# Retention steps at fixed distances, the sum of squares later, background work at every fourth step, later last loads

## The chip, the cores and the metric

The kernel runs on one core of one Trainium2 chip, as one launch. The metric is the device time of an execution in microseconds. The engines go by their names in the profile: PE is TensorE, DVE is VectorE, ACT is ScalarE, POOL is GpSimd, SP issues most DMAs.

## The reference

One layer of a streaming encoder on 512 frames of width 2048, in float32 (cut to what matters):

```python
h = rmsnorm(x, norm_gain)
proj = h @ w_in
(aq, ak, av, az, iq, ik, iw, rq, rk, rv, rz, ga, gb) = jnp.split(proj, SPLIT_POINTS, axis=-1)
ik = plain_layernorm(ik)
a_out = dsa_mixer(aq, ak, av, iq, ik, iw, positions, rel_bias) * jax.nn.silu(az)   # top-128 keys
rq, rk = rope(rq, positions), rope(rk, positions) * (R_KEY_DIM ** -0.5)
b_out = retention_mixer(rq, rk, rv, ret_gn_gain) * jax.nn.silu(rz)
merged = jax.nn.sigmoid(ga) * (a_out @ w_a_out) + jax.nn.sigmoid(gb) * (b_out @ w_b_out)
r = x + merged @ w_o
return r + (p_i @ w_ple) * jax.nn.sigmoid(r @ w_ple_gate)      # and a last rmsnorm
```

The retention mixer has 8 heads of width 128. For each head and chunk it takes scores of turned queries and keys with a decay, adds what the state of earlier chunks gives, and normalises each frame's output over the head (a group norm).

## The kernel before

**Matmuls in split parts.** A float32 product is made of reduced-precision matmuls. Every weight block arrives by DMA as `wraw`; ACT copies it into a high part `wh` (L138), and DVE (or POOL in the retention and attention stages) subtracts to get the low part `wl` (L144). A plain gemm (`gemms`, L198 to L200) issues three matmuls of 512 columns for each 128 of the inner dimension; a gate pair (`gemm_pair`, L253 and L254) makes two output blocks with seven products of eight times two matmuls, by a Strassen-like scheme whose moving parts are prepared sums (`hd` in DRAM, 56 tiles).

**Steps set the order.** No scheduler reorders anything: the instructions stand in program order on each engine. After every group of matmuls the code calls `step()`. A step first runs whatever `later(n, f)` has put on that step, then takes one entry of the list `todo`; an entry of `None` does nothing. If the step's entry is `None` or the list is empty, and the number of the step is a multiple of `state["rate"]` (`BG_RATE`, 3 at first), one background piece is issued from `bg`. So the list is a sequence in which work waits for its turn behind what was listed earlier, and `later` is a fixed distance.

**Stages.** The stages around the change, with the steps each gives:

- The first gemm (keys and head weights of the indexer), 32 steps, with x split and the squares of x summed in two accumulators. Then `f_sum` (L449, DVE, adds the two), `f_rnat` (L394, four one-column matmuls `ps_ms` over the partitions, then the reciprocal root), `f_bcast`, `f_keys1` to `f_keys3`, all in `todo`, during seven index gemms of 16 steps each. The index scores follow in the same list, 9 entries for each gemm.
- The values for heads 0 to 3 (64 steps), then heads 0 to 3 of 32 steps each: the queries' gemm (`ps_rq`), their rotation on DVE (L719 to L722), the keys' gemm (`ps_rk`), their rotation. Then the values for heads 4 to 7 and these heads.
- A retention head's twelve further steps run inside the next head's gemms: `scores` (L752, four matmuls that need the rotated keys, then DVE's L754), `keys` (a turn on PE and a copy on ACT), `states` (L775, L777, L779), `values_out` four times (L789, L791), `norm` (statistics on DVE, L796 to L800, and a power on POOL, L801), `scale` (L808, `yn`), `back` (L762 turns `yn` on PE, L817 copies it as `yT`; two steps later SP stores it, L818). They stand in `todo`: 35 entries with their gaps.
- Head 7 makes queries and keys together and calls `x_load(2)` sixteen times: SP loads moving parts of the gates back from `hd` (L832) into tiles that the normalised x lets go. With ten loaded at its start this makes 42 of 56. The last 14 are put on fixed steps after head 7.
- The gate pairs, 56 steps each. The first runs beside the steps of head 7. Later stages are not touched.

**Background.** The pieces are, in order: for 8 pairs of blocks of x a load, a normalisation (L649) and four steps that make the gates' moving parts (L268, L277 to L280) and store them to `hd`; 48 top-k rounds (L606, L607, L609); 160 pieces for the position bias. There are 256 in all. In the gates the rate is 24.

**Tiles.** Most tiles come from one pool of 65 slots of 128 by 512 (`U`). A new tile gets the free slot that was let go first, and its first writer waits until the old tile's last reader is done.

Of the kernel before, what the change touches and what calls it, by code (L numbers as in the profile page):

```python
# [19 lines left out]
NH = 8  # L20
NT = L // 128
# [13 lines left out]
def block_kernel(tc, xT, pT, posb, posq, w_in, w_v, w_ik, w_a, w_b, w_o, w_ple, w_gate,  # L35
# [4 lines left out]
    with contextlib.ExitStack() as ctx:  # L40
# [10 lines left out]
        def U(name, dt=F32):  # L51
            return up.tile([128, L], dt, name=name, tag="u")

        def B(name, dt=F32):
            return bp.tile([128, 1280], dt, name=name, tag="b")

        def P(name):
            return pp.tile([128, L], F32, name=name, tag="p")

        def S(name, n):  # L60
            return sm.tile([128, n], F32, name=name, tag=f"s{n}")

        def tok(t):
            return slice(128 * t, 128 * t + 128)
# [6 lines left out]
        unfinished = {}  # L71
        state = {"raw": 0, "split": 0, "rate": BG_RATE}
        pool_units = []
# [82 lines left out]
        todo = collections.deque()  # L156
# [4 lines left out]
        def later(n, f):  # L161
            if n <= 0:
                return f()
            tick[1] += 1
            heapq.heappush(soon, (tick[0] + n, tick[1], f))
# [176 lines left out]
        for k in range(KT):  # L342
            if k in (1, 2, 4, 8, 12):
                load_to(state["raw"] + 1)
            if k < 10:
                t = U("xk")
                sp.dma_start(t, xT[:, k, :])
                xs.append(t)
            elif k % 2 == 0:
                t = B("xk2")  # L350
# [201 lines left out]
            dve.scalar_tensor_tensor(st[64:128, :], st[64:128, :], -1.0, r_b[64:128, :], op0=OP.mult, op1=OP.mult)  # L552

        N3 = [None] * 3
        todo.extend(N3 * 2 + [f_sum] + N3 + [f_rnat] + N3 * 3 + [f_bcast, None, f_keys1] + N3 * 3 + [f_keys2] + N3 * 2 + [f_keys3] + N3 * 2)
        later(80, f_pos)
        later(96, f_rope1)
        later(104, lambda: f_turns(0))
# [166 lines left out]
        def retention_head(h, vs):  # L725
# [6 lines left out]
            else:  # L732
                i = u_r[h][0][0]
# [24 lines left out]
            def turn(src, n):  # L758

                ps = P("ps_t")  # L760
                for t in range(n):
                    pe.transpose(ps[:, tok(t)], src[:, tok(t)], ident)  # L762
                return ps[:, 0:128 * n]

            def keys(i):
                if i == 0:
                    E["pk"] = turn(sk, 3)
                else:
                    E["kn"] = U("kn")
                    act.activation(E["kn"][:, 0:384], E["pk"], AF.Copy, scale=dect[:, 256:257])  # L770
# [12 lines left out]
            def values_out(t):  # L783
                if t == 0:
                    E["py"] = P("ps_y")
                    E["st"] = S("gst", 24)
                    E["mv"] = S("gmv", 8)
                o = E["py"][:, tok(t)]
                pe.matmul(o, E["at"][:, tok(t)], vs[t][:, hc], start=True, stop=(t == 0))  # L789
                if t:  # L790
                    pe.matmul(o, qd[:, tok(t - 1)], E["s"][:, tok(t - 1)], start=False, stop=True)  # L791
# [20 lines left out]
            def back(i):  # L812
                if i == 0:
                    E["pt"] = turn(E["yn"], NT)
                else:
                    E["yT"] = U("yT")
                    act.activation(E["yT"], E["pt"], AF.Copy, scale=gn[:, h:h + 1])  # L817
                    later(2, lambda: sp.dma_start(yd[h], E["yT"]))  # L818

            todo.extend([None] * 5)  # L820
            todo.extend([scores, lambda: keys(0), None, lambda: keys(1)] + [None] * 3 + [states, None, None])
            todo.extend([lambda t=t: values_out(t) for t in range(NT)])
            todo.extend([None, norm] + [None] * 5 + [scale] + [None] * 5 + [lambda: back(0), None, lambda: back(1)])

        Xh = {n: [None] * 8 for n in PRODUCTS}
        x_wanted = collections.deque((n, k) for n in PRODUCTS for k in range(8))
# [1 line left out]
        def x_load(count):  # L828
            while x_wanted and count:
                n, k = x_wanted.popleft()  # L830
                Xh[n][k] = U("h" + n, F32R)
                sp.dma_start(Xh[n][k].bitcast(F32), x_at[n, k])  # L832
                count -= 1

        for h in range(NH):
            if h % 4 == 0:
                rv = values(u_rv[h // 4], "rv")
            retention_head(h, rv)
        for i in range(len(x_wanted)):
            later(4 + 2 * i, lambda: x_load(1))  # L840
        hparts.clear()
        state["rate"] = BG_RATE2

# [199 lines left out]
        for m in PAIRED:  # L1043
            t = B("sm")
# [18 lines left out]
        for m in range(8):  # L1063
# [13 lines left out]
            if m == 7:  # L1077
                todo.extend([None] * 24)
                for k in range(2):
                    t = U("pk")  # L1080
# [9 lines left out]
        for m in range(MF):  # L1090
            i = u_p[m // 4][0]
# [3 lines left out]
            h, l = loaded[i]  # L1095
# [8 lines left out]
            t = U("pw")  # L1104
# [158 lines left out]
IN_RAWS = 2  # L1263
AHEAD = 4
LOADS = 5
BG_RATE = 3
BG_RATE2 = 24
X_AHEAD = 10
AZ_PAIRED = 4
# [98 lines left out]
```

## Time and profile before

| | us |
|---|---|
| median of three runs | 1810.67 (1810.29 to 1814.06) |
| the profiled execution, its own time | 1809.38 |
| its span in the trace | 1807.6 |
| PE busy | 1752.1 (97%) |
| DVE busy | 1210.6 (67%) |
| ACT busy | 738.1 (41%) |
| POOL busy | 395.4 (22%) |
| mean granted TensorE clock | 0.99 of full speed |

The index gemms run from about 28 us to 104 us of the span, the first values to 155 us, heads 0 to 3 to 257 us, the second values to 305 us, heads 4 to 7 to 404 us, the gate pairs to about 873 us. A row of the waits names the waiting engine, tile and line, then what ended the wait, then the total, the number and the longest in us. A row of a timeline has the start, the duration, the engine, the line, the operation and its shapes; in brackets stands the idle time before it and what ended that.

### The profile page before, as it was taken

To read this page: it belongs to the slowest core of one execution; us is meant where nothing else is said; L and a number is where in the kernel's file an instruction comes from. 1 tells how busy PE (TensorE), PEld (TensorE's weight loads), DVE (VectorE), ACT (ScalarE), POOL (GpSimd) and SP (SyncE) were. 2 spreads that over 40 slices of the span, in tenths; PEclk is the share of its full clock that TensorE was granted. 3 is DMA by queue.
4 is the path that set the end of the run, shared out by engine and by line. 5 is a ranking of instruction groups with operands and counts; after the bars stand their busy time and mean duration, and the time that the engine had idled before them with its cause. 6 is when DMAs were issued, how large, how long until landed. Compare 5 with 4: busy or idle time off the path is not lost. (4 is left out here: it accounts for less than half of the span.)

```text
span 1807.6 us, 23881 instructions
## 1 busy us (share of the span) xinstructions
PE 1752.1 (97%) x8966; PEld 1462.5 (81%) x8966; DVE 1210.6 (67%) x1959; ACT 738.1 (41%) x1087; POOL 395.4 (22%) x262
## 2 busy tenths in 40 slices
PE   9999999998999999999999999998989999999997
PEld 7988788887888888888777777886778888878887
DVE  8787874867776667776765357547557878774453
ACT  7464332224444545444532333333334443463332
POOL 2002344432321111110000144354310011111222
PEclk9999999999999999999999999999999999999999
DMA  7327652389878877778875423333236578753312
GB/s 280 110 101 265 227 189 98 102 286 290 231 196 208 209 201 206 201 198 202 295 251 178 135 96 104 106 108 117 71 107 206 161 212 205 174 175 105 94 59 93
DMA packets 114580, 309.65 MB, mean 171 GB/s; under 512 B 12832, under 2 KB 21024, under 8 KB 114464
## 3 DMA queue, kind: packets, MB, share of 16 engines
q1 hardware_dynamic: 91072, 244.15, 40.1%
q0 software_dynamic: 13600, 49.29, 14.7%
q10 hardware_dynamic: 9792, 14.68, 2.4%
q8 instruction: 70, 1.15, 0.3%
q14 instruction: 46, 0.38, 0.1%
HBM read 266.14 MB, written 41.94 MB: 170 GB/s over the span
## 5 line engine op out<-in xcount | busy, mean ns | idle before, releaser
L138 ACT ACTIVATE wh<-wraw 128x1024 fp32r<-128x1024 f32 (+2 forms) x404 | 415.5, 1043 | 535.3 <-issue 100.0
L144 DVE TENSOR_TENSOR wl<-wraw,wh 128x1024 fp32r<-128x1024 f32 (+2 forms) x324 | 401.7, 1243 | 258.7 <-ACT wh L138 258.3
L144 POOL TENSOR_TENSOR wl<-wraw,wh 128x1024 fp32r<-128x1024 f32 x80 | 192.6, 2410 | 339.8 <-ACT wh L138 243.2
L106 POOL DMA_DIRECT2D wraw<-w_in x66 | 58.9, 955 | 366.9 <-DVE wl L144 255.3
L253 PE MATMUL ps_r<-hs,wh 128*128 128x512 f32 x352 | 127.9, 402 | 3.7 <-DVE e_d L232 3.4
L694 PE MATMUL ps_vn<-wh,hh 128*128 128x512 f32 x256 | 102.1, 399 | 0.0
L695 PE MATMUL ps_vn<-wl,hh 128*128 128x512 f32 x256 | 100.1, 391 | 0.0
L696 PE MATMUL ps_vn<-wh,hl 128*128 128x512 f32 x256 | 99.8, 390 | 0.0
L254 PE MATMUL ps_r<-hs,wl 128*128 128x256 f32 x352 | 99.0, 281 | 0.2 <-DVE wl L144 0.2
L253 PEld LDWEIGHTS ps_r<-hs,wh 128*128 128x128 f32 x352 | 66.0, 188 | 23.9 <-issue 8.2
L198 PE MATMUL ps_pg<-rh,wh 128*128 128x512 f32 x192 | 74.7, 389 | 0.0
L199 PE MATMUL ps_pg<-rl,wh 128*128 128x512 f32 x192 | 74.7, 389 | 0.0
L200 PE MATMUL ps_pg<-rh,wl 128*128 128x512 f32 x192 | 74.7, 389 | 0.0
L254 PEld LDWEIGHTS ps_r<-hs,wl 128*128 128x128 f32 x352 | 66.5, 189 | 1.1 <-DVE wl L144 1.0
L106 POOL DMA_DIRECT2D wraw<-w_o x24 | 21.1, 933 | 206.8 <-DVE wl L144 179.2
L709 DVE STREAM_TRANSPOSE bm<-pn 32x320 f32<-32x320 f32 x128 | 64.3, 503 | 1.9
L253 PE MATMUL ps_v<-hs,wh 128*128 128x512 f32 x176 | 65.0, 407 | 0.0
L253 PE MATMUL ps_v<-ha,wh 128*128 128x512 f32 x176 | 63.7, 397 | 0.0
L253 PE MATMUL ps_q<-ha,wh 128*128 128x512 f32 x176 | 63.3, 399 | 0.0
L253 PE MATMUL ps_p<-hs,wh 128*128 128x512 f32 x176 | 63.3, 398 | 0.0
L253 PE MATMUL ps_p<-ha,wh 128*128 128x512 f32 x176 | 63.3, 399 | 0.0
L917 POOL TENSOR_TENSOR bm<-bm,mneg 128x1280 f32<-128x1280 f32 x8 | 21.7, 2708 | 182.1 <-DMA bm<-scr 182.1
(389 smaller groups left out, 4709.3 us busy)
## 6 DMA issues: line engine op xcount, KB each, us to landing
wraw<-w_in SPq DMA_DIRECT2D x174, 512.0 KB, 4.4
wraw<-w_in POOLq DMA_DIRECT2D x66, 512.0 KB, 7.9
wraw<-w_v SPq DMA_DIRECT2D x32, 512.0 KB, 3.9
wraw<-w_o SPq DMA_DIRECT2D x32, 512.0 KB, 4.3
wraw<-w_o POOLq DMA_DIRECT2D x24, 512.0 KB, 7.7
wraw<-w_gate SPq DMA_DIRECT2D x24, 512.0 KB, 4.3
hd<-hs SPq DMA_DIRECT2D x32, 256.0 KB, 2.4
hs<-hd SPq DMA_DIRECT2D x32, 256.0 KB, 5.9
```

The lines of the kernel that those rows point to most:

```text
L106: pool.dma_start(out=raw_tiles[r], in_=src[:, k0:k0 + 8, :], accum_op=OP.add)
L138: act.activation(h, raw, AF.Copy)
L144: e.tensor_sub(l, raw, h.bitcast(F32))
L198: pe.matmul(o, h[:, k, w], a, start=(s == order[0]), stop=False)
L199: pe.matmul(o, h[:, k, w], b, start=False, stop=False)
L200: pe.matmul(o, l[:, k, w], a, start=False, stop=(s == order[-1]))
L253: pe.matmul(o, h[:, k], x, start=(n < 4 and k == 0), stop=False, skip_group_check=True)
L254: pe.matmul(o[:, LO], l[:, k], x[:, LO], start=False, stop=(k == 7), skip_group_check=True)
L694: pe.matmul(pss[t], a[:, tok(t)], h[:, k], start=(s == 0), stop=False)
L695: pe.matmul(pss[t], a[:, tok(t)], l[:, k], start=False, stop=False)
L696: pe.matmul(pss[t], b[:, tok(t)], h[:, k], start=False, stop=(s == KT - 1))
L709: dve.transpose(out=d[32 * a:32 * a + 32, :, 32 * b:32 * b + 32], in_=f[32 * b:32 * b + 32, :, 32 * a:32 * a + 32])
```

## The change

Five edits:

- The list before the index scores gets 9 more empty entries: three ahead of `f_sum` and six between `f_sum` and `f_rnat`.
- A head's twelve steps leave `todo` and go on fixed distances from the end of its keys' gemm. In the old list without delay the distances were 6, 7, 9, 13, 16, 17, 18, 19, 21, 27, 33, 35 steps.
- Head 7 has distances of its own, 24 to 82, that reach into the second gate pair; heads 0 and 4 have `scores` at 8.
- The last 14 loads of moving parts stand at steps 20, 22, ..., 46 after head 7 and not at 4, 6, ..., 30.
- Background pieces come at every fourth step and not at every third; as `todo` is empty in retention now, no listed step displaces one.

```diff
-        todo.extend(N3 * 2 + [f_sum] + N3 + [f_rnat] + N3 * 3 + [f_bcast, None, f_keys1] + N3 * 3 + [f_keys2] + N3 * 2 + [f_keys3] + N3 * 2)
+        todo.extend(N3 * 3 + [f_sum] + N3 * 3 + [f_rnat] + N3 * 3 + [f_bcast, None, f_keys1] + N3 * 3 + [f_keys2] + N3 * 2 + [f_keys3] + N3 * 2)
...
-            todo.extend([None] * 5)
-            todo.extend([scores, lambda: keys(0), None, lambda: keys(1)] + [None] * 3 + [states, None, None])
-            todo.extend([lambda t=t: values_out(t) for t in range(NT)])
-            todo.extend([None, norm] + [None] * 5 + [scale] + [None] * 5 + [lambda: back(0), None, lambda: back(1)])
+            at = (24, 26, 30, 38, 44, 46, 48, 50, 54, 66, 78, 82) if h == NH - 1 else \
+                (8, 9, 11, 15, 18, 19, 20, 21, 23, 27, 32, 34) if h % 4 == 0 else \
+                (6, 7, 9, 13, 16, 17, 18, 19, 21, 26, 32, 34)
+            for n, f in zip(at, (scores, lambda: keys(0), lambda: keys(1), states,
+                                 *(lambda t=t: values_out(t) for t in range(NT)), norm, scale,
+                                 lambda: back(0), lambda: back(1))):
+                later(n, f)
...
         for i in range(len(x_wanted)):
-            later(4 + 2 * i, lambda: x_load(1))
+            later(20 + 2 * i, lambda: x_load(1))
...
-BG_RATE = 3
+BG_RATE = 4
 BG_RATE2 = 24
```

## The prediction

> **What bounds the kernel now.** I read the page first, then TensorE's waits over the whole span, then windows around the three waits that the change can reach, then the timelines inside them.
>
> ```profile
> PE 1752.1 (97%) x8966; PEld 1462.5 (81%) x8966; DVE 1210.6 (67%) x1959; ACT 738.1 (41%) x1087; POOL 395.4 (22%) x262
> ```
>
> TensorE is the bound: 1752.1 of 1807.6 us. No matmul goes, so all that can be had is its idle time, 55.5 us, and the time that it runs at a lowered clock.
>
> ```profile
> PE ps_t L762 <- DVE yn L808: 5.2, 1, 5.2
> PE ps_b L1242 <- POOL rl L1238: 3.7, 1, 3.7
> PE ps_ms L394 <- DVE sq L449: 2.9, 1, 2.9
> PE ps_rs L752 <- DVE ra L722: 2.5, 1, 2.5
> ```
>
> Three of these rows are steps that the change moves: `ps_ms` (sum of squares), `ps_rs` (a head's scores), `ps_t` from `yn` (a head's output turned back). Each occurs once. The windows hold one of them each; the fourth row is a gate pair without one.
>
> ```profile
> 43.92:53.24 9.32, 6.41 (x23) 6.24 (x23) 5.86 (x10) 2.03 (x3) 1.04 (x1) 0.63 0.34 114
> 176.64:190.00 13.36, 10.82 (x56) 8.86 (x54) 10.59 (x13) 3.18 (x5) 5.51 (x3) 1.00 0.69 232
> 404.15:436.52 32.37, 27.16 (x152) 23.63 (x151) 25.58 (x48) 12.36 (x17) 4.83 (x5) 0.89 0.89 295
> 436.52:456.52 20.00, 19.98 (x114) 17.13 (x113) 13.24 (x17) 9.70 (x12) 5.79 (x6) 1.00 0.95 283
> ```
>
> The number before the DMA share is the granted clock: 0.63 and 0.89 in the first and third windows, 1.00 in the second. Two of the three waits cost clock as well as idle time.
>
> **Part 1, the sum of squares.** f_sum goes 3 steps later, f_rnat and all behind it 9.
>
> ```profile
> 43.75 0.34 PE L200 MATMUL ps_iq<-hh,wl 128*128 128x384 f32 x1
> 47.01 1.86 PE L394 MATMUL ps_ms<-ones,sq 128*128 128x1 f32 x8 [2.92 <-DVE sq L449]
> 48.73 0.67 PE L198 MATMUL ps_iq<-hh,wh 128*128 128x384 f32 x1
> ...
> 53.24 0.34 PE L200 MATMUL ps_iq<-hh,wl 128*128 128x384 f32 x1
> ...
> 56.02 1.05 PE L405 MATMUL ps_bc<-cs,r_nat 128*128 128x128 f32 x8
> ```
>
> From 53.24 to 56.02 run 16 matmuls, 0.174 us each; from 48.73 to 53.24 only 14 intervals fit, 4.51 us instead of 2.43. Three matmuls make a step, 0.52 us, so nine steps put the ms matmuls 4.7 us later, which is more than the 2.92 us they waited. VectorE's order up to f_sum stays as it is, since the next gemm's splits are issued behind both places. Gone: 2.92 idle, 2.08 of slow matmuls, and 0.81 of ms itself (1.86 against the 1.05 of eight larger ones at full clock), together 5.8 us. What comes later (r_nat, the keys' normalisation, the index scores) spills nine steps further into the first values stage, which has 64 steps; I cost that at nothing, and 0.5 us if the cover fails.
>
> The Trainium skill ("TensorE: Matmul & The Clock Gate", HAM oscillation) wants no TensorE gap above about 3.4 us. By that rule a gap of 2.92 would keep the clock, and this part would be worth 2.9 us instead of 5.8. The trace disagrees: the granted clock was 0.63 here, perhaps because matmuls of one column follow the gap.
>
> **Part 2, scores at 6 steps after the keys, 8 for heads 0 and 4.** Head 4 shows what six steps are now:
>
> ```profile
> 326.58 0.39 PE L200 MATMUL ps_rk<-hh,wl 128*128 128x512 f32 x1
> ...
> 331.06 1.13 PE L752 MATMUL ps_rs<-ra 128*128 128x128 f32 x8
> ```
>
> ```profile
> 329.14 1.78 DVE L722 TENSOR_TENSOR ra<-ra,rb 128x512 f32<-128x512 f32 x1
> ```
>
> Its keys end at 326.97, the turned keys are there at 330.92 (3.95 us), the scores start at 331.06 without a wait: six steps are 4.1 us, 0.68 each, and cover the turn by 0.1. Head 0 is the one that waited:
>
> ```profile
> 176.41 0.39 PE L200 MATMUL ps_rk<-hh,wl 128*128 128x512 f32 x1
> ...
> 183.43 0.82 PE L752 MATMUL ps_rs<-ra 128*128 128x128 f32 x5 [2.54 <-DVE ra L722]
> ```
>
> ```profile
> 178.02 2.62 DVE L268 TENSOR_TENSOR ha<-xn,ha 128x256 fp32r<-128x256 f32 x1
> ...
> 182.68 0.69 DVE L722 TENSOR_TENSOR ra<-ra,rb 128x512 f32<-128x512 f32 x1
> ```
>
> Keys end at 176.80, turned keys at 183.37: 6.6 us. The subtraction at 178.02 belongs to the fifth background piece between the two rotations; at every fourth step there are four, and the scores come two steps (1.4 us) later. So 2.5 us gone.
>
> The other heads lose slack: heads 1, 2, 3, 5 and 6 had 9, 12, 15, 9 and 12 steps. Head 2 shows what that slack hid:
>
> ```profile
> 230.44 0.39 PE L200 MATMUL ps_rk<-hh,wl 128*128 128x512 f32 x1
> ```
>
> ```profile
> 232.26 2.40 POOL L144 TENSOR_TENSOR wl<-wraw,wh 128x1024 fp32r<-128x1024 f32 x1 [2.62 <-ACT wh L138]
> ```
>
> ```profile
> 232.71 2.57 DVE L268 TENSOR_TENSOR hs<-t,hs 128x256 fp32r<-128x256 f32 x2
> ...
> 237.32 0.69 DVE L722 TENSOR_TENSOR ra<-ra,rb 128x512 f32<-128x512 f32 x1
> ```
>
> From 230.83 to 238.01 are 7.2 us, because a subtraction stood from 232.71 until POOL's split ended at 234.66. So a background operation still open about 1.4 us after the keys costs the scores 7.2 - 4.2 = 3.0 us.
>
> The Trainium skill ("SBUF — State Buffer", on the shared port pair) says that a VectorE operation with two SBUF inputs and a GpSimd operation that reads SBUF exclude each other for a whole instruction. That speaks against short distances, and the trace agrees: 2.57 us for two small subtractions beside POOL's 2.40.
>
> Which heads are at risk I counted from step numbers: between the rotations the new order gives head 1 what it has now, head 2 less than now, and head 3 the set (one norm, three splits, statistics, scale) that head 2 has now; heads 5 and 6 have four top-k pieces, as before. Head 3's scale comes two pieces earlier, so its last piece may clear POOL's split. I take 1.0 us for all five, nearest to head 4's row; bounds 0 and 15.0 (five times 3.0).
>
> **Part 3, the first gate pair.** In the kernel before, the 35 listed steps of a head outlast the 32 steps of the next, so each head of a group of four starts 3 steps later. Head 6 begins 6 steps late; its scale is issued after head 7's two rotations and two weight splits.
>
> ```profile
> 411.98 1.34 PE L762 MATMUL ps_t<-cs,yn 128*128 128x128 f32 x4 [5.21 <-DVE yn L808]
> ```
>
> ```profile
> 408.55 0.69 DVE L722 TENSOR_TENSOR ra<-ra,rb 128x512 f32<-128x512 f32 x1
> 409.15 2.35 DVE L144 TENSOR_TENSOR wl<-wraw,wh 128x1024 fp32r<-128x1024 f32 x2
> 411.42 1.36 DVE L808 TENSOR_SCALAR yn<-ps_y,gmv,grs 128x128 f32<-128x128 f32 x4
> ```
>
> At the new distances (scale at 26, back at 32) both steps lie before the rotations, in head 7's own gemms, six steps (4.1 us) apart against 1.36 us of work. The 5.21 goes. The clock of 0.89 over 32.37 us stands for at most 3.6 us more. Check: 27.16 busy, less the 20.00 of a pair without retention steps, less 3.6, leaves 3.6 for the 39 small matmuls that lie in this pair, 0.09 each. So up to 8.8 us.
>
> What is late next: (a) the weight split for the pair's third unit ends at about 410.3 (first of the two at 409.15). A gate step is 20.00/56 = 0.357 us, and without the wait TensorE needs that split at step 16, 404.15 + 5.7 = 409.9, hence 0.4 us. (b) The last 14 loads of moving parts. They move past head 6's store on SP's queue, and one weight load passes them.
>
> ```profile
> SPq L818 <- ACT yT L817: 18.8, 3, 7.4
> SPq L832 <- DMA hs<-hd: 9.0, 13, 2.8
> SPq L832 <- PE ps_y L789: 1.9, 1, 1.9
> ```
>
> ```profile
> hs<-hd SPq DMA_DIRECT2D x32, 256.0 KB, 5.9
> ```
>
> SP stood up to 7.4 us behind that store; now the store is released as the pair begins. But the last three loads are issued at steps 42, 44 and 46 and get tiles let go between steps 40 and 46, as the third row shows for one before; the product that needs the last of them follows step 55. Nine steps are 3.2 us, with small matmuls between 3.8 us; the median landing is 5.9 us, under a queue kept full. Bounds: 0 if the queue is no longer full, 2.1 us at the median. I take 0.6, nearer the lower end, because SP gets the early ones of the 14 out while it stood still before. Net gain of part 3: 7.8 us, bounds 6.3 and 8.8.
>
> **Part 4, background pieces.** Rate 4 without gaps gives 90 pieces by the end of head 7, rate 3 around the listed steps 95. Five top-k pieces move into the gates, where VectorE is waited for already:
>
> ```profile
> PE ps_v L254 <- DVE wl L144: 5.3, 12, 0.6
> ```
>
> Five times at most 0.6 us: 0 to 3.0 us; I take 0.5, the lower half, since VectorE is busy only 67% of the span. The other pieces keep their number per head within two.
>
> **Sum** against the profiled execution (1809.38 us, of it 1.8 around the span): -5.8 - 2.5 + 1.0 - 7.8 + 0.5 = -14.6 us, 1794.8. The median of the runs is 1.3 us above that execution, so the forecast is 1796.1.
>
> **Rivals.** 1, the loads take the place of the wait: the moving parts of the last product land late. For it: DMA share 0.89 in the window and SP's row of 9.0 us waiting for landings; against it: SP's 7.4 us standstill goes. Price: a wait of 3 us and a slow clock again, at most 3.6 us, so 6.6, less the 0.6 counted: 1796.1 + 6.0 = 1802.1.
>
> 2, slower: scores wait. If heads 1, 2, 3, 5 and 6 all meet head 2's case, five waits of 3.0 us follow, each with the 2.1 us of slow matmuls that the 2.92 us wait brought: 25.5 us in place of the 1.0, so 1796.1 + 24.5 = 1820.6. It decides from four heads on (20.4 - 1.0 against 14.6). For it: 3.95 us stand against 4.1. Against it: in the trace only two of eight heads go beyond 5 us, and neither's neighbour does. By the skill's rule on gaps (part 1) the clock would hold: 1796.1 + 14.0 = 1810.1, no change; the 1.00 at head 0's 2.54 us wait agrees so far.
>
> **How the numbers follow.** Forecast 0.65, with 1792.5 to 1800 as its own range; rival 1 0.2; rival 2 0.09 with the slow clock, 0.06 without or with three heads only. The range 1792 to 1805 holds the forecast and rival 1: its lower end is the whole gain of 17.1 us without any of the costs, 1793.6, less the 1.3 between one execution and the median; its upper end is three heads waiting 3.0 us each, 1796.1 + 8.0, rounded up. A difference of 0.2%, 3.6 us, is about what a measurement of this kernel can tell from no change. Faster 0.85, same 0.06, slower 0.09.
>
> **What would show it.** Right: the rows for `ps_ms`, `ps_rs` and `ps_t` gone from TensorE's waits, the clock at 1.00 around 45 and 400 us, the first gate pair 23 to 25 us long instead of 32.37. Part 3 fails if `ps_r` or `ps_v` waits for `hs<-hd` there. Part 2 fails if `ps_rs` waits for `ra` more than once, at about 3 us. Part 1 fails if `ps_ms` still waits, or the wait shows at the next step that needs r_nat. More than 3 us of added waits for `wl` or `e_d` in the gates would show part 4 mis-sized.

## The result, and the profile after

The changed kernel took 1801.6 us, median of five runs (1800.6 to 1805.37), beside 1811.84 us (1810.29 to 1817.65) for the kernel before: a ratio of 0.994, 95% interval 0.9922 to 0.9958. The gain is 10.2 us; 14.6 was forecast. On two other chips the same kernel came out at 0.9956 (0.9941 to 0.9971) and 0.9953 (0.9935 to 0.9971), some 7 us. The profiled execution took 1800.6 us.

The page of after, and TensorE's waits over the span (in total, times, longest, in us):

```profile
PE 1749.2 (97%) x8966; PEld 1461.3 (81%) x8966; DVE 1207.8 (67%) x1959; ACT 739.3 (41%) x1087; POOL 394.5 (22%) x262
```

```profile
PE ps_v L254 <- DVE wl L144: 5.9, 13, 0.6
PE ps_r L253 <- DMA hs<-hd: 5.9, 3, 2.6
PE ps_r L253 <- DVE e_d L232: 4.8, 11, 1.7
```

The rows for `ps_ms`, `ps_rs` and `ps_t` are gone. A new one stands there: the last product of the first gate pair waits for its moving parts. The windows of after, at the places of those before (the number before the DMA share is the granted clock):

```profile
43.92:53.24 9.32, 9.32 (x58) 9.32 (x57) 7.12 (x11) 3.09 (x4) 1.04 (x1) 1.00 0.64 193
176.64:190.00 13.36, 13.36 (x75) 11.45 (x74) 10.73 (x15) 4.50 (x9) 5.91 (x3) 1.00 0.61 204
395.29:425.58 30.29, 24.41 (x147) 20.93 (x145) 23.97 (x41) 12.16 (x16) 6.90 (x7) 0.95 1.05 350
425.58:447.97 22.39, 22.39 (x117) 19.09 (x117) 17.80 (x28) 10.83 (x13) 5.21 (x6) 0.91 0.70 213
```

The first two are full now, at full clock. The first gate pair takes 30.29 us instead of 32.37, but the second takes 22.39 without any idle time, at a clock of 0.91, instead of 20.00: together 52.68 us, before 52.37. Inside, on TensorE's timeline:

```profile
418.48 0.50 PE L253 MATMUL ps_r<-hs,wh 128*128 128x512 f32 x1 [0.82 <-DMA hs<-hd]
...
421.55 0.50 PE L253 MATMUL ps_r<-hs,wh 128*128 128x512 f32 x1 [2.45 <-DMA hs<-hd]
...
424.77 0.80 PE L253 MATMUL ps_r<-hs,wh 128*128 128x512 f32 x1 [2.61 <-DMA hs<-hd]
```

The third matmul takes 0.80 us instead of 0.50: the clock has fallen, and the next 16 (from 425.58 to 430.36) take 4.8 us instead of about 3.

Where the span's 8.8 us came from, by the start of stages in the two traces: up to the first gate pair 404.15 became 395.29 (-8.9); the first two pairs +0.3; the other gate pairs, which end at 862.8 us instead of 874.0, -2.7; all behind them +2.4. The last two need care: from one profiled execution of the same changed kernel to the next (three were taken) all the gate pairs together differ by 5 us (467.5, 463.9 and 462.0), while the place at which they start differs by 0.3.

### The profile page after: what moved, and what is told of

Same layout as the page of the kernel before. It is cut to its first block, busy times and chain, and to the rows that moved or that the text cites. A ratio compares the mean times of both kernels' runs of the same rounds, so it can differ in the third digit from the quotient of the medians.

```text
span 1798.8 us, 23890 instructions
## 1 busy us (share of the span) xinstructions
PE 1749.2 (97%) x8966; PEld 1461.3 (81%) x8966; DVE 1207.8 (67%) x1959; ACT 739.3 (41%) x1087; POOL 394.5 (22%) x262
```

## The experiments

The question: why did the first gate pairs give back what the change took out of them, and which edit made the gain? Theory 1: the last loads of moving parts are issued too late by their place. Theory 2: the queues are full there, whatever the place. There are three series, each on a chip of its own beside the kernel before, whose medians were 1803.28, 1802.77 and 1802.43 us. Times of different series are compared by their ratios; differences within a series have a 95% interval from resampling the runs.

**First series: the changed kernel with single edits.** Earlier loads:

```diff
-            later(20 + 2 * i, lambda: x_load(1))
+            later(8 + 2 * i, lambda: x_load(1))
```

> The changed kernel with its last 14 loads of moving parts at steps 8, 10, ..., 34 after head 7 instead of 20, ..., 46. Theory 1, the loads are late because of their place and the tiles they wait for: the last three are issued some 12 steps (4.3 us) earlier, the 5.9 us that the first gate pair waits for hs shrinks to 1.6 us or less and the half clock behind it goes: 6 to 7 us less than the changed kernel. Theory 2, they are late because the queue is full: the same bytes stand in the same queue, the wait stays at 4 us or more, within 2 us of the changed kernel.

Measured: 1789.45 us, ratio 0.9925 (0.990 to 0.995). Its wait, and the first two pairs as windows:

```profile
PE ps_r L253 <- DMA hs<-hd: 2.5, 2, 1.8
```

```profile
395.35:422.97 27.62, 25.09 (x147) 0.96 1.05 356
422.97:444.21 21.24, 21.24 (x118) 0.97 0.87 263
```

The place of the loads counts: 48.9 us for the two pairs instead of 52.7. The wait lies between what the two theories named (1.6 us or less, 4 or more), and the clock is not full.

Head 7's steps closer, loads where they were before:

```diff
-            at = (24, 26, 30, 38, 44, 46, 48, 50, 54, 66, 78, 82) if h == NH - 1 else \
+            at = (15, 16, 18, 22, 25, 26, 27, 28, 30, 36, 42, 44) if h == NH - 1 else \
...
-            later(20 + 2 * i, lambda: x_load(1))
+            later(4 + 2 * i, lambda: x_load(1))
```

> The changed kernel with head 7's steps (15 to 44) and the last loads (4 to 30) where the kernel before had them, all else as changed. Theory 1 (place and tiles): no wait for hs in the first gate pair, 6 to 8 us less than the changed kernel, unless back, six gate steps (2.1 us) behind scale, waits for yn: then up to 3 us of that come back. Theory 2 (queue full): the wait for hs stays above 4 us, within 2 us of the changed kernel.

Measured: 1791.55 us, ratio 0.9926 (0.990 to 0.9952). No wait for `hs`; a new one of 1.85 us for head 7's turned keys; the two pairs take 46.9 us. The last three loads are issued at 409.5 to 412.8 us, in after at 413.2 to 414.7. Two things differ here, the distances and the place of the loads, and loads from step 4 on with the wide distances weren't tried: how much belongs to the distances stays open.

The background rate:

```diff
-BG_RATE = 4
+BG_RATE = 3
```

> The changed kernel with background pieces at every third step. Theory: the fourth step is what keeps VectorE clear at the ends of the keys; with five or six pieces between the rotations instead of four, at least two of heads 0 to 3 wait 1 to 3 us for their turned keys: 3 to 12 us more than the changed kernel. Rival: the distances alone removed the wait at head 0, no scores wait, within 2 us.

Measured: 1802.17 us, ratio 0.9998 (0.9984 to 1.0012). All is lost. Heads 1 and 2 wait for their turned keys, as the theory said, by 0.8 and 1.8 us. TensorE's waits:

```profile
PE ps_r L253 <- DMA hs<-hd: 7.2, 4, 3.1
...
PE ps_rs L752 <- DVE ra L722: 2.6, 2, 1.8
```

The first two gate pairs take 58.7 us, 5.7 more than in the next kernel, on the same chip; the difference of the medians is 7.4 (3.8 to 9.6). Why these pairs take longer at rate 3 isn't shown.

The old list of the sum of squares:

```diff
-        todo.extend(N3 * 3 + [f_sum] + N3 * 3 + [f_rnat] + N3 * 3 + [f_bcast, None, f_keys1] + ...
+        todo.extend(N3 * 2 + [f_sum] + N3 + [f_rnat] + N3 * 3 + [f_bcast, None, f_keys1] + ...
```

> The changed kernel with the sum of squares, and what follows it in the list, at its old places. Theory: the 2.9 us wait and the half clock behind it come back, 5.8 us more than the changed kernel. Rival, by the rule that only gaps above 3.4 us lower the clock: 2.9 us more, the clock at 1.00 behind the wait.

Measured: 1794.78 us, ratio 0.9956 (0.994 to 0.9972): no dearer than the change itself. In its trace the wait of `ps_ms` is back (2.9 us), with a granted clock of 0.82 in the window from 43.92 to 53.24 us (0.63 in before), and the gate pairs start 4.7 us later than in after. So the mechanism of the theory is there, without its price, and the rival's full clock is not.

**Second series: queue or place.** The changed kernel itself, unchanged:

> The changed kernel, unchanged, on the same chip as the three others. Expected a ratio of 0.994 to the kernel before, the wait of ps_r for hs<-hd of 5 to 6 us in the first gate pair, that pair 30 us long, and heads and first values as in its first profile (gates start at 395 us).

Measured: 1795.7 us, ratio 0.9956 (0.9941 to 0.9971), `hs` waited for 6.4 us. Its first two pairs as windows:

```profile
395.44:428.28 32.84, 26.06 (x147) 0.89 1.05 355
428.28:450.24 21.96, 21.96 (x118) 0.93 0.64 189
```

The issues of its DMAs between 404 and 424 us (times, KB each, median us to landing), and above them the queues (packets, MB, share of 16 engines); q0 carries what GpSimd issues:

```profile
q1 hardware_dynamic: 2475, 5.18, 68.8%
q0 software_dynamic: 388, 1.46, 36.5%
...
hs<-hd SPq DMA_DIRECT2D x8, 256.0 KB, 9.2
wraw<-w_in SPq DMA_DIRECT2D x4, 512.0 KB, 12.4
wraw<-w_in POOLq DMA_DIRECT2D x3, 512.0 KB, 8.3
```

The DMA engines are full (68.8% and 36.5%). GpSimd's transfers, nearly all of them additions to a weight block already loaded, take 25% of the engines for each MB, SP's 13%. The loads of moving parts need 9.2 us instead of the 5.9 that I took from the page of before.

Those additions left out in the first pair:

```diff
         def add_block(r, b):
+            if state.get("no_add"):
+                return
             src, k0 = b
...
         state["rate"] = BG_RATE2
+        state["no_add"] = True
...
             gate_pair(u, AF.Silu, b_out)
+            state["no_add"] = False
```

> The changed kernel without the adding weight DMAs that GpSimd issues during the first gate pair (the sums of weight blocks that they form are left out, the loads stay at steps 20 to 46). Theory 1 (place): the last loads are issued at 413 to 415 us as before, landings fall by at most 1 us, the wait for hs<-hd stays at 5 to 6 us. Theory 2 (the queue is full, the adds above all): the landing of the last three loads falls from 7 to 10 us to about 5 to 6 us and the wait to below 2 us, the time 3 to 5 us below the changed kernel.

This kernel leaves out sums that the result needs, so only its time counts. Measured: 1785.57 us, ratio 0.9907 (0.9885 to 0.9928), 10.1 us (6.6 to 12.3) below the changed kernel, where theory 2 had expected 3 to 5. Its issues in the same stretch, its wait, and its first two pairs as windows:

```profile
q1 hardware_dynamic: 3023, 6.78, 95.5%
q0 software_dynamic: 44, 0.15, 1.9%
...
hs<-hd SPq DMA_DIRECT2D x8, 256.0 KB, 5.1
```

```profile
PE ps_r L255 <- DMA hs<-hd: 1.5, 1, 1.5
```

```profile
395.44:420.63 25.19, 23.71 (x146) 1.00 1.01 366
420.63:441.24 20.61, 20.61 (x118) 1.00 0.76 226
```

With the loads at their late place, the wait falls from 6.4 to 1.5 us and the clock holds: 45.8 us for the two pairs, where the changed kernel on this chip took 54.8. By the windows 5.3 of these 9.0 us are idle time of TensorE, and 3.7 are busy time, at the lower clock. The last three loads are issued at 413.3 to 414.3 us and land 3.9 to 5.9 us later; in the changed kernel they are issued at 413.5 to 415.8 and land 10.8 to 11.8 us later. The engines are as busy here (95.5% and 1.9%) as with the additions, so it isn't a full queue as such that makes the landings long, but the additions in it. With them the late place costs (theory 2); with the loads at 8 in the first series less of the cost is left although the additions stay (theory 1).

The loads at 8 again, now beside the changed kernel:

> The changed kernel with the last 14 loads at steps 8, 10, ... instead of 20, 22, ..., beside the changed kernel on one chip. Theory 1 (the loads come late by their place): a wait for hs<-hd of 2 to 3 us instead of 6, the first pair 26 to 27 us instead of 30, and the whole 3 to 6 us (0.2 to 0.3%) below the changed kernel. Theory 2 (the queues are full whatever the place): the same wait and the same time within 1.5 us.

Measured: 1791.87 us, ratio 0.9938 (0.9915 to 0.996), 3.8 us (0.9 to 6.0) below the changed kernel. No wait for `hs` in this execution; TensorE went on and met the next late step:

```profile
PE ps_t L762 <- DVE yn L808: 5.0, 1, 5.0
...
PE ps_kv L775 <- ACT kn L770: 1.4, 1, 1.4
```

On VectorE's timeline:

```profile
424.70 1.23 DVE L144 TENSOR_TENSOR wl<-wraw,wh 128x1024 fp32r<-128x1024 f32 x1
429.99 1.35 DVE L144 TENSOR_TENSOR wl<-wraw,wh 128x1024 fp32r<-128x1024 f32 x1 [4.07 <-ACT wh L138]
431.38 1.22 DVE L146 TENSOR_TENSOR wraw<-wraw 128x1024 f32<-128x1024 f32 x1
432.52 1.36 DVE L808 TENSOR_SCALAR yn<-ps_y,gmv,grs 128x128 f32<-128x128 f32 x4
```

Head 7's scale (`yn`) stands behind a weight split that waits 4.07 us for a weight block, held up by the same queue: the block's addition was issued at 419.44 us and landed 9.4 us later.

The old list of a head's steps, loads at 4, the other edits kept:

```diff
-            at = (24, 26, 30, 38, 44, 46, 48, 50, 54, 66, 78, 82) if h == NH - 1 else \
...
-                later(n, f)
+            todo.extend([None] * 5)
+            todo.extend([scores, lambda: keys(0), None, lambda: keys(1)] + [None] * 3 + [states, None, None])
+            todo.extend([lambda t=t: values_out(t) for t in range(NT)])
+            todo.extend([None, norm] + [None] * 5 + [scale] + [None] * 5 + [lambda: back(0), None, lambda: back(1)])
```

> The changed kernel with the twelve steps of a head back in the list (with its gaps) and the last loads back at 4, 6, ...; the sum of squares late and one background piece every fourth step stay. By the prediction's part 3 the wait of ps_t for yn comes back with 4 to 6 us, the first pair is 31 to 33 us long, no wait for hs<-hd; the wait of ps_rs for ra at head 0 stays away or is under 1 us if four pieces instead of five caused its going, and is 2.5 us if the two steps of distance did. The time is 4 to 9 us above the changed kernel. Rival: the drift of three steps for each head cost nothing of its own, and the time is within 2 us of the changed kernel, whose wait for hs<-hd takes the place of it.

Measured: 1800.27 us, ratio 0.9983 (0.9969 to 0.9997), 4.6 us (1.7 to 7.6) above the changed kernel. The wait for `yn` is back as predicted, with no wait for `hs`:

```profile
PE ps_r L253 <- DVE e_d L232: 10.8, 15, 1.7
...
PE ps_t L762 <- DVE yn L808: 5.2, 1, 5.2
```

But its first two pairs take 50.9 us, less than the changed kernel's, so the loss lies behind them. The top-k rounds in the gate pairs are 25 of 48:

```profile
L606 DVE MAX8 m<-isc x25: 418/554/691, 424.0 to 641.4; 128x8 f32<-128x512 f32 x9, 128x8 f32<-128x256 f32 x8, 128x8 f32<-128x384 f32 x8
```

Between the entries of the list, a rate of 4 leaves few steps for background pieces. The wait for `e_d`, VectorE's own work, is 10.8 us, where the changed kernel on that chip had 6.5. That the 25 rounds cause it is argued, not shown, and the two profiled executions differ by only 1.0 of the 4.6 us.

**Third series: what made the gain.** The yardstick:

> The changed kernel again, as the yardstick on the chip of the next three. Expected 0.994 to 0.9956 of the kernel before, gates from 395 us, 5 to 7 us of waits for hs<-hd.

Measured: 1795.54 us, ratio 0.9953 (0.9935 to 0.9971).

The loads at 8, and head 7's scale ahead of the split that held it:

```diff
-            at = (24, 26, 30, 38, 44, 46, 48, 50, 54, 66, 78, 82) if h == NH - 1 else \
+            at = (24, 26, 30, 40, 45, 47, 49, 51, 54, 62, 78, 82) if h == NH - 1 else \
...
-            later(20 + 2 * i, lambda: x_load(1))
+            later(8 + 2 * i, lambda: x_load(1))
```

> The changed kernel with the last 14 loads at steps 8, 10, ... and head 7's steps at (24, 26, 30, 40, 45, 47, 49, 51, 54, 62, 78, 82): the state two steps later, the scale four steps earlier, so that it is issued ahead of the weight split that waits for its load at the start of the second pair. Theory (the yn wait of 5.0 us in the second pair with the loads at 8 comes from the scale's place behind that split): no wait of ps_t for yn and none of ps_kv for kn, hs<-hd at most 2.5 us, the second pair at full clock; 4 to 8 us below the changed kernel. Rival (the queues set the pace of both pairs, whichever step is late): the 3 to 5 us come back as waits for wl or hs, and the time is within 2 us of the changed kernel with the loads at 8, about 3 to 4 us below the changed kernel.

Measured: 1790.58 us, ratio 0.9931 (0.9906 to 0.9955), 5.0 us (0.7 to 9.4) below the changed kernel. The waits for `yn` and `kn` are gone; `hs` is waited for 2.5 us, and the clock fell (0.97 and 0.88 in the two windows):

```profile
394.70:422.30 27.60, 25.06 (x147) 0.97 1.05 355
422.30:444.77 22.47, 22.47 (x117) 0.88 0.79 237
```

That it beats the loads at 8 alone is not shown (0.9925 and 0.9938): the rival, that the queue sets the pace whichever step is late, stands. The two kernels with the loads at 8 that ran beside the changed kernel beat both it and the kernel before, by 4 to 5 and by 11 to 12 us.

The old list of the sum of squares again, beside the changed kernel:

> The changed kernel with the old list of the sum of squares, beside the changed kernel on one chip. Theory 1 (part 1 is worth its 5.8 us to the end): gates start 5 us later, and the time is 4 to 6 us above the changed kernel. Theory 2 (the full queues take it back: with less time ahead of them the first gate pairs lose no more): the gates start 5 us later, and the time is within 2 us of the changed kernel.

Measured: 1794.87 us, ratio 0.9955 (0.9938 to 0.9972), 0.7 us below the changed kernel (3.8 below to 2.9 above). In the trace the gate pairs start at 401.6 instead of 395.2 us, as theory 1 said. The time is the one of theory 2, but its reason doesn't show: the first two pairs take 53.6 us here and 53.7 in the changed kernel, so nothing is given back in them.

The new list of the sum of squares alone, in the kernel before:

> The kernel before with the new list of the sum of squares alone. Theory 1: head 0 starts 5.8 us earlier, the waits of ps_rs (2.5) and ps_t (5.2) stay, and the time is 5 to 6 us below the kernel before (ratio 0.997). Theory 2: head 0 starts 5.8 us earlier, but the time is within 2 us of the kernel before, the rest being given back in retention or the first gate pairs.

Measured: 1793.39 us, ratio 0.9941 (0.9921 to 0.996): as much as the whole change, 2.1 us below it (6.4 below to 1.9 above). Its windows at the sum of squares and at the first pair, and its one wait at a step of retention:

```profile
43.92:53.24 9.32, 9.32 (x58) 1.00 0.60 201
...
395.70:428.00 32.30, 27.10 (x153) 0.89 0.90 297
```

```profile
PE ps_t L762 <- DVE yn L808: 5.2, 1, 5.2
```

The first pair is the one of before, wait, slow clock and all. Yet it starts at 395.7 us, 8.5 earlier than before: 6.0 of it are there when head 0 starts (148.9 instead of 154.9), and 2.5 come from head 0, whose scores don't wait here either, although they are where they were before.

## Why the prediction was right, and where it was wrong

**Part 1** (-5.8) held in the trace: head 0 starts 5.8 us earlier (154.9 to 149.1) and the window is at clock 1.00. That edit alone, with head 0's 2.5 us that came along, made the time 9 us shorter. What stays open is why taking it back costs nothing: two traces without it start the gates 4.7 and 6.4 us later, and the medians of two series don't show it. The profiled executions of that kernel were the longest of their series (1799.85 and 1802.13 against medians of 1794.78 and 1794.87), so the traces may not show what the other executions did.

**Part 2** (-2.5 + 1.0) came out as -2.5 and 0: no head's scores wait, so rival 2 found no place. But its reason was too narrow. The new list of the sum alone ends head 0's wait, at rate 3 and the old distance, and so do the other edits without it. In both traces the subtraction ahead of head 0's second rotation takes 0.4 us instead of 2.62, as it no longer falls beside a weight split on GpSimd. The 2.5 us is had once, by either.

**Part 3** (-7.8) failed, and with it the sum. The mechanism was right: the wait for `yn` goes with the new distances and comes back with the old list. The failing step is the size of cost (b), the last 14 loads, which I put at 0.6 with bounds of 0 and 2.1: 5.9 us of waiting and some 2 us of clock. The steps of its working: I took the median landing of before over its whole span (5.9 us) as the worst case. Over the span it is 6.0 in after, but for the eight loads issued between 404 and 424 us it is 7.4 (9.2 on another chip), and the last three, issued within 1.5 us, need 5.2, 7.4 and 10.1. SP itself also stands behind landings and tiles. Its waits between 380 and 430 us, in after:

```profile
SPq L836 <- DMA hs<-hd: 8.1, 11, 2.8
...
SPq L836 <- DVE go L858: 2.5, 1, 2.5
...
SPq L836 <- PE ps_y L789: 1.6, 2, 1.1
```

The first row is hardly longer than in the kernel without the additions (7.9 us), so SP's waits don't explain the difference; the additions do. Without them the two pairs take 45.8 us; the prediction's 52.37 - 7.8 is 44.6. So 6.6 of the 7.8 us were there to be had, and the queue took them. What the prediction overlooked: the wait for `yn` seems to have kept the additions away from the loads. The kernel before with the new list alone starts its gates at the same time and still waits; between 404 and 424 us it moves 0.57 MB on GpSimd's queue, with a median landing of 4.9 us for `hs`, where after moves 1.47 MB. This is rival 1: its mechanism, and nearly its price (6.6 us, of waiting and slow clock; 7.9 measured). It named 1802.1 us, and 1801.6 came; that they agree to half a microsecond is luck, since the gain ahead of the gates and the price both came out over a microsecond larger. I gave it 0.2, by counting SP's standstill for the loads and not asking what else is on the queue at their new place.

**Part 4** (+0.5): the count was right, 42 top-k rounds ahead of the gates instead of 47. Its price can't be told from the rest, but the rate isn't a matter of half a microsecond: with fixed distances rate 3 loses all the gain (0.9998 against 0.9956), with the list rate 4 loses most of what the sum gives (0.9983 against 0.9941). Distances and rate only go together.

So the time is inside the range for a reason other than the likeliest case: the gain came ahead of the gates, 8.9 us where 7.3 was forecast, and the four other edits together add nothing to the first that these runs can show. Nor does the first add anything to those four (0.9956 and 0.9955 without it): why the two gains don't add up stays open.

**The clock.** The Trainium skill ("TensorE: Matmul & The Clock Gate", HAM oscillation) puts the limit at a single gap of about 3.4 us. After disagrees again: no gap above 2.61 us, and the clock fell to 0.91 in the second pair. No matmul of one column follows here, so the prediction's guess at part 1 isn't needed for it.

## What to carry to other kernels

Before a load is moved later, list what the DMA queues carry at its new place, GpSimd's transfers too: a median landing holds for the place where it was read. A wait that goes is worth its length only if the next late thing has another cause; where one busy queue feeds all of them, take bytes or costly transfers off it first. And try each edit of a bundle alone: here one line gave what five did, and the other four gave as much without it.

## What the runs showed of the hardware

- An addition by DMA costs the engines about twice what a plain load does for each MB: 36.5% for 1.46 MB beside 68.8% for 5.18 MB. The addition and not GpSimd's queue seems to cost it: with the additions left out, the little that is left on that queue takes 1.9% for 0.15 MB, 13% for each MB like SP's.
- The TensorE clock falls after waits that are short but close together: 0.82, 2.45 and 2.61 us within 7 us gave 0.91 in the next window, 1.80 and 0.70 us within 2 us gave 0.97 with the loads at 8, while single waits of 1.48 us (additions left out) and of 2.54 us (head 0 before) left it at 1.00. A small wait a little earlier is enough: 1.98 us gave 0.76 in the next 7 us when 0.34 us had been waited 4.8 us before (changed kernel, third series), and 1.00 when it was 0.11 us (second series).
- The same single wait costs more clock in one execution than in another: 2.91 us before `ps_ms` gave 0.63 in the kernel before, and 0.82 and 0.70 in the two traces of the changed kernel with the old list, in the window from 43.92 to 53.24 us.
- Up to the first gate pair the changed kernel's trace repeats within 0.3 us (395.29, 395.44 and 395.16 in three profiles), but with the old list of the sum, whose wait lowers the clock, the gates start at 400.04 and 401.56; 460 us later, at the end of the gate pairs, the changed kernel's traces lie within 6 us (862.8, 859.3, 857.2).
